# Stick-breaking attention on one core: the softplus total of later keys carried in one row of the next key block

## The chip, the cores and the metric

The kernel runs on one core of a Trainium2 chip. The metric is the device time of one execution in microseconds (us); for the kernel before, three runs gave 1367.43, 1368.22 and 1368.27, median 1368.22. A profile is one further execution, taken by the hardware profiler. In it, PE is TensorE (matmuls), PEld its weight loads, DVE VectorE, ACT ScalarE, POOL GpSimd, SP SyncE, which here only issues DMAs.

## The reference

One layer of a hybrid decoder: 1024 tokens, width 1024, everything in float32. A combined projection gives queries, keys and values (8 heads of 64), three inputs of a short convolution and two gates; both branches are merged, projected and normalised, and a feed-forward part follows. The change lies in the attention:

```python
z = jnp.einsum("bhqd,bhkd->bhqk", qb, kb).astype(jnp.float32) * scale
...
strict = s_idx < t_idx
log_keep = jnp.where(strict, jax.nn.log_sigmoid(-z), 0.0)
later = lax.cumsum(log_keep, axis=3, reverse=True) - log_keep
w = jnp.where(strict, jnp.exp(jax.nn.log_sigmoid(z) + later), 0.0)
outs.append(jnp.einsum("bhqk,bhkd->bhqd", w, vb.astype(jnp.float32)))
```

With sp(z) = log(1 + exp(z)), the weight of key s for query t is exp(z - S), where S is the sum of sp over the keys from s up to t - 1: the key itself and all later ones.

## The kernel before

Precision is kept by splitting each float32 operand into two 16-bit halves, high and low, and multiplying three of the four pairs (PASSES, L35). So most tiles that go into a matmul are made by two instructions: a copy on ACT (the high half) and a subtraction on DVE (the low half).

**Stages.** build() (L206) makes the constants, among them tri (L252 to L257): tri[:, 0] is 1 where the summed key is at or behind the key of the output row, tri[:, 1] its complement. mixer() (L264) loads and normalises the tokens x, transposes them into hT, projects v into four tiles v16 (v_out, L331), and q and k for four pairs of heads (qk_tile, L280; pair j holds two heads on 64 partitions each). The start, up to L501, has its order on PE, DVE and ACT written out by hand. Then come the four attention(j) (L591), after them the branches, the gates and the output projection, and ffn() (L990).

**Attention.** One pair has 12 units: for each half c of the queries (512 of them) the key blocks i of 128 keys, from the last that the half can see down to 0. A unit's tiles have 128 keys on the partitions and 2 x 512 columns (two heads, 512 queries); blocks on the diagonal are narrower by off (L595), so that the widths of both heads together are 256, 512, 768 and 1024 columns, then 1024 for all blocks below. stage1 (L602) makes z on PE, zc = min(scaled z, 44) with the causal mask on DVE, sp by Exp and Ln on ACT, and its halves sh. stage2 (L629) adds tri[:, 0] x sh to the PSUM tile A, which then holds S, makes zc - A on DVE, exp of it on ACT, and the halves w. stage2b (L647) adds the complement tri[:, 1] x sh, so that A holds the whole block's total in every row, ready for the next block. stage3 (L655) multiplies with v into o, which is copied into two halves o16 when a query half is finished (L668, L669).

**Order.** Program order is made by merge (L693): the loop at L673 runs stage1 of unit k, stage2 of unit k - 1, stage2b, and stage3 of unit k - 2, and between them it lets generators emit other matmuls: v tiles, q and k of the next pair, the convolution's inputs, in the last pair the first gate and four tiles of a branch (L707 to L720). What each engine runs in which order is then settled when the program is built, by a scheduler that keeps a timeline of its own and goes by priorities (high_priority at L609, L660, L675 to L685); an engine runs its list from front to back. Tiles come from pools with a fixed number of buffers: z, A and o have one, sp, sh and w two, zc three. A new tile waits until the last reader of the buffer's old tile is done. The table set that ACT uses for Exp and Ln together is loaded at L240; the sigmoid of the first gate (L786) and the gelu (L1240) use other sets. The weights' loads wait in SP's queue in program order.

Of the kernel before, what the change touches and what calls it, by code (L numbers as in the profile page):

```python
# [16 lines left out]
F16 = mybir.dt.float16  # L17
BF16 = mybir.dt.bfloat16
F32 = mybir.dt.float32
I32 = mybir.dt.int32  # L20
AF = mybir.ActivationFunctionType
ALU = mybir.AluOpType
AX = mybir.AxisListType

P = 128
# [9 lines left out]
PASSES = ((0, 0), (0, 1), (1, 0))  # L35


class Layer:
# [167 lines left out]
    def build(self):  # L206
# [23 lines left out]
        with ExitStack() as top:  # L230
# [24 lines left out]
            self.tri = c.tile([P, 2, P], F16, tag="tri", name="tri")  # L255
            nc.vector.tensor_copy(self.tri[:, 0, :], tri32)
            nc.vector.tensor_scalar(self.tri[:, 1, :], tri32, -1.0, 1.0, ALU.mult, ALU.add)  # L257
# [6 lines left out]
    def mixer(self, mid):  # L264
        tc, nc, a = self.tc, self.nc, self.a
        hT = self.hp.tile([P, 2, KD, T], F16, tag="hT", name="hT")
        with ExitStack() as ph1:
# [4 lines left out]
            self.clamp = att.tile([P, 2, NH], F16, tag="clamp", name="clamp")  # L272
            nc.gpsimd.memset(self.clamp, 44.0)
            nc.gpsimd.affine_select(self.clamp[:, :, :P], self.clamp[:, :, :P], [[0, 2], [1, P]], ALU.is_gt,
                                    -30000.0, base=0, channel_multiplier=-1)
            v16 = [self.slot([P, 2, 4, 4, 64], F16, f"v16_{i}") for i in range(4)]

            stk = {}

            def qk_tile(j, which):  # L280
# [12 lines left out]
                if which == "k":  # L293
                    cz = self.small(f"cz{j}", keep=True)
                    self.mul(cz[:, 0:1], s["iq"], inv)
                    self.mul(cz[:, 1:2], cz[:, 0:1], cst[:, 0:1])
                    s["cz"] = cz[:, 1:2]
# [3 lines left out]
            with tc.tile_pool(name="ptp", bufs=2, space=bass.MemoryType.PSUM) as ptp:  # L301
# [36 lines left out]
                def v_tile(tt):  # L338
# [9 lines left out]
                    v_out(tt, pv)  # L348

# [60 lines left out]
                with tc.manual_schedule(engines={ET.PE, ET.DVE, ET.Activation}):  # L410
# [51 lines left out]
                    v_out(1, pv[1])  # L462
                    square_x(5)
# [16 lines left out]
                    v_out(3, pv[3])  # L480
                    low(5)
# [109 lines left out]
            def attention(j):  # L591
# [10 lines left out]
                def stage1(u):  # L602
# [9 lines left out]
                    zc = att.tile([P, 2, NH], F32, tag="zc", name=f"zc{nm}", bufs=3)  # L612

                    if u["diag"]:
                        nc.vector.scalar_tensor_tensor(zc[:, :, off:], z[:, :, off:], s["cz"],  # L615
                                                       self.clamp[:, :, :NH - off], ALU.mult, ALU.min)
                    else:
                        nc.vector.tensor_scalar(zc[:, :, off:], z[:, :, off:], s["cz"], 44.0,
                                                ALU.mult, ALU.min)

                    sp = att.tile([P, 2, NH], F32, tag="sp", name=f"sp{nm}", bufs=2)
                    nc.scalar.activation(sp[:, :, off:], zc[:, :, off:], AF.Exp)  # L622
                    nc.scalar.activation(sp[:, :, off:], sp[:, :, off:], AF.Ln, bias=self.one)  # L623
# [3 lines left out]
                    u["zc"], u["sh"] = zc, sh  # L627

                def stage2(u):  # L629
                    off, i, c, nm, sh, zc = u["off"], u["i"], u["c"], u["nm"], u["sh"], u["zc"]  # L630
                    if u["top"]:
                        acc["A"] = pat.tile([P, 2, NH], F32, tag="A", name=f"A{nm}")
                    A = acc["A"]
                    for h in range(2):
                        for hl in range(2):
                            mm(A[:, h, off:], self.tri[:, 0, :], sh[:, hl, h, off:],
                               start=u["top"] and hl == 0, stop=False)
                    nc.vector.scalar_tensor_tensor(zc[:, :, off:], A[:, :, off:], -1.0, zc[:, :, off:],  # L638
                                                   ALU.mult, ALU.add)
                    nc.scalar.activation(zc[:, :, off:], zc[:, :, off:], AF.Exp)  # L640
                    w = att.tile([P, 2, 2, NH], F16, tag="w", name=f"w{nm}", bufs=2)
                    nc.scalar.activation(w[:, 0, :, off:], zc[:, :, off:], AF.Copy, scale=2.0 ** 14)  # L642
# [643 lines left out]
```

## Time and profile before

| | us |
|---|---|
| median of three runs | 1368.22 |
| the profiled execution, span from first to last instruction | 1365.7 |
| PE busy in the span | 1336.1 |
| DVE busy | 1028.6 |
| ACT busy | 860.7 |
| DVE low halves of sh (L626), 48 of them | 45.7 |
| DVE zc - A (L638), 48 of them | 45.5 |
| ACT Ln (L623), 48 of them | 44.6 |
| ACT exp (L640), 48 of them | 40.0 |

The span leaves out what lies before the first and behind the last instruction; the median of the runs is 2.5 us above it. A row of the timeline reads: start, duration, engine, line, operation, tile written <- tiles read, shape, number of instructions merged into the row, and in brackets how long the engine sat idle before it and what ended that. Numbers of buffers and pairs are left out of tile names, so zc stands for the zc of any unit. A row of a view by stretches reads: from:to, length, then the busy time of each engine with its number of instructions.

### The profile page before, as it was taken

How to read it: one execution, taken by the hardware profiler on the slowest of the kernel's cores; microseconds unless marked ns; L12 is line 12 of the kernel's file. 1: busy time of each engine (PE TensorE's matmuls, PEld its weight loads, DVE VectorE, ACT ScalarE, POOL GpSimd, SP SyncE). 2: the span in 40 equal slices, each digit the busy share in tenths (PEclk: the TensorE clock that was granted, in tenths of full speed). 3: DMA queues.
4: the chain of work that ended last, by engine and by line, in shares of the span. 5: the costliest groups of instructions: out<-in, count | busy, mean ns of one | idle time of the engine just before them, and what ended most of it. 6: DMA issues, size and time to landing. Idle time of an engine off the chain costs nothing. (4 is left out here: it accounts for less than half of the span.)

```text
span 1365.7 us, 16990 instructions
## 1 busy us (share of the span) xinstructions
PE 1336.1 (98%) x6651; PEld 607.7 (44%) x6651; DVE 1028.6 (75%) x1610; ACT 860.7 (63%) x1204; POOL 34.2 (3%) x52
## 2 busy tenths in 40 slices
PE   6999999999999999999999999999999999999997
PEld 3444444444444444444454444444444444444443
DVE  6667777777775965878788985984894896699855
ACT  6668778787775775666466577652761673476524
POOL 2000000000000000000010000000000000000002
PEclk9999999999999999999999999999999999999999
DMA  7102111101111121351331123122220321313216
GB/s 264 62 1 62 32 31 32 38 25 39 40 31 47 32 62 31 93 185 36 119 124 62 62 62 123 39 87 85 70 78 16 123 62 62 109 45 124 63 46 109
DMA packets 26576, 96.06 MB, mean 70 GB/s; under 512 B 3072, under 2 KB 3200, under 8 KB 26496
## 3 DMA queue, kind: packets, MB, share of 16 engines
q1 hardware_dynamic: 25056, 89.74, 20.3%
q0 software_dynamic: 1440, 5.24, 2.1%
q8 instruction: 52, 0.85, 0.2%
q14 instruction: 28, 0.23, 0.1%
HBM read 86.58 MB, written 8.39 MB: 70 GB/s over the span
## 5 line engine op out<-in xcount | busy, mean ns | idle before, releaser
L1156 PEld LDWEIGHTS <-wh_u 128*128 128x128 f16 x1848 | 178.8, 98 | 217.3 <-issue 3.5
L1048 PE MATMUL pd<-wdh,f 128*128 128x512 f16 (+1 forms) x1068 | 230.3, 377 | 2.8 <-ACT wdh L86 1.2
L1048 PEld LDWEIGHTS <-f 128*128 128x128 f16 x1068 | 104.4, 98 | 127.2 <-issue 4.3
L86 ACT ACTIVATE wh_u<-ws_u,sc 128x1024 f16<-128x1024 f32 (+1 forms) x66 | 64.7, 998 | 102.9 <-DVE sc L78 79.3
L1055 DVE SCALAR_TENSOR_TENSOR yacc<-pd,sd,yacc 128x512 f32<-128x512 f32 (+1 forms) x81 | 58.5, 740 | 72.7 <-PE pd L1048 65.2
L1156 PEld LDWEIGHTS <-wh_g 128*128 128x128 f16 x588 | 56.9, 98 | 68.7 <-issue 0.4
L859 PE MATMUL py<-wh_wo,m 128*128 128x512 f16 x384 | 83.9, 379 | 0.0
L87 DVE SCALAR_TENSOR_TENSOR wh_u<-ws_u,sc,wh_u 128x1024 f16<-128x1024 f32 (+1 forms) x66 | 72.1, 1099 | 9.5 <-ACT wh_u L86 9.4
L643 DVE SCALAR_TENSOR_TENSOR w<-zc,w 128x1024 f16<-128x1024 f32 (+3 forms) x48 | 45.7, 955 | 34.5 <-ACT w L642 34.4
L622 ACT ACTIVATE sp<-zc 128x1024 f32<-128x1024 f32 (+3 forms) x48 | 40.2, 838 | 46.7 <-DVE zc L615 29.1
L600 PE MATMUL A<-sh,tri 128*128 128x512 f16 (+3 forms) x352 | 67.8, 322 | 0.0
L1233 DVE SCALAR_TENSOR_TENSOR ugu<-cgu,cw_g,ugu 128x1023 f32<-128x1023 f32 (+1 forms) x44 | 56.2, 1278 | 11.3 <-ACT ugu L1231 10.9
L1233 DVE SCALAR_TENSOR_TENSOR ua<-cau,cw_a,ua 128x1023 f32<-128x1023 f32 (+1 forms) x44 | 56.1, 1276 | 1.4 <-ACT ua L1231 1.3
L859 PEld LDWEIGHTS <-m 128*128 128x128 f16 x384 | 37.5, 98 | 44.1
L626 DVE TENSOR_TENSOR sh<-sp,sh 128x1024 f16<-128x1024 f32 (+3 forms) x48 | 45.7, 952 | 12.9 <-ACT sh L625 12.7
L640 ACT ACTIVATE zc<-zc 128x1024 f32<-128x1024 f32 (+3 forms) x48 | 40.0, 834 | 15.4 <-DVE zc L638 15.0
L638 DVE SCALAR_TENSOR_TENSOR zc<-A,zc 128x1024 f32<-128x1024 f32 (+3 forms) x48 | 45.5, 949 | 2.3 <-PE A L600 2.3
L56 ACT ACTIVATE jk_u<-ws_u 128x1024 bf16<-128x1024 f32 x44 | 46.4, 1054 | 0.9
L200 PE MATMUL pk<-hT,wh_k 128*128 128x512 f16 x192 | 46.8, 380 | 0.0
L200 PE MATMUL pq<-hT,wh_q 128*128 128x512 f16 x192 | 44.3, 379 | 1.3 <-DVE sc L79 1.3
L623 ACT ACTIVATE sp<-sp,one 128x1024 f32<-128x1024 f32 (+3 forms) x48 | 44.6, 928 | 0.8
L200 PE MATMUL pcb<-hT,wh_cb 128*128 128x512 f16 x192 | 44.8, 379 | 0.0
(620 smaller groups left out, 2606.4 us busy)
## 6 DMA issues: line engine op xcount, KB each, us to landing
ws_u<-w_up_nt SPq DMA_DIRECT2D x44, 512.0 KB, 3.7
ds<-w_down SPq DMA_DIRECT2D x22, 512.0 KB, 6.1
wd<-w_down SPq DMA_DIRECT2D x22, 512.0 KB, 3.7
ws_g<-w_in_nt SPq DMA_DIRECT2D x14, 512.0 KB, 3.6
x<-x SPq DMA_DIRECT2D x8, 512.0 KB, 8.0
ws_wo<-w_out SPq DMA_DIRECT2D x8, 512.0 KB, 7.1
xr<-x SPq DMA_DIRECT2D x8, 512.0 KB, 4.3
out<-x SPq DMA_DIRECT2D x7, 512.0 KB, 2.9
```

The lines of the kernel that those rows point to most:

```text
L56: self.nc.scalar.activation(self.junk(f"jk_{name}"), src, AF.Square, accum_out=acc)
L86: self.nc.scalar.activation(dst[:, 0, :], src, AF.Copy, scale=s)
L87: self.nc.vector.scalar_tensor_tensor(dst[:, 1, :], src, s, dst[:, 0, :], ALU.mult, ALU.subtract)
L200: nc.tensor.matmul(ps, w[:, wi, ds(k * P, P)], hT[:, hi, k, ds(c * NH, NH)], start=n == 0, stop=n == last)
L600: nc.tensor.matmul(out, w, mv, skip_group_check=True, **kw)
L626: nc.vector.tensor_tensor(sh[:, 1, :, off:], sp[:, :, off:], sh[:, 0, :, off:], ALU.subtract)
L643: nc.vector.scalar_tensor_tensor(w[:, 1, :, off:], zc[:, :, off:], 2.0 ** 14, w[:, 0, :, off:], ALU.mult, ALU.subtract)
L859: nc.tensor.matmul(ps, m16[k][:, hi, ds(tt * P, P)], wo[k][:, wi, sl], start=k == 0 and p == 0, stop=k == 7 and p == 2)
L1048: nc.tensor.matmul(pd[nh], f16[g][k][:, hi, ds(tt * P, P)], w[k][:, wi, ds(*part)], start=run is runs[0] and n == 0, stop=run is runs[-1] ...
L1055: nc.vector.scalar_tensor_tensor(y[:, sl], ps, sm[:, 0:1], y[:, sl], ALU.mult, ALU.add)
L1156: nc.tensor.matmul(ps, w[wt][:, wi, ds(wc * NH + k * P, P)], self.block(i, hi, k), start=first and n == 0, stop=n == 3 * KH - 1, skip_grou ...
L1233: nc.vector.scalar_tensor_tensor(u[:, lag:], c[:, :T - lag], sm[:, 2 - lag:3 - lag], u[:, lag:], ALU.mult, ALU.add)
```

## The change

The order of two keys is changed in each block of 128: key 127, the last one, is put in row 96, and key 96 in row 127. For k this is a swap of two columns with three small copies on DVE; for v the two rows go out to DRAM and come back crossed, four DMAs for each of the four tiles. tri and the causal mask are built for this order, tri without its complement. As key 127 is the last of its block, what stands in its sp row enters the sums of all other rows. So the total of all later blocks, which is row 0 of their A, is added to row 96 of the next block's sp, and A is made anew for each unit by four matmuls. The weight is now the product of e = min(exp(z), 1.2e19) and g = exp(-A), where 1.2e19 stands for the old bound of 44 in the exponent. ACT takes exp(z) directly from the PSUM tile of z. In the loop, stage2 of unit k - 1 now stands ahead of a new stage1b of unit k, which adds the row and makes sh. e has three buffers, and g shares the two buffers of sp.

```diff
@@ -33,6 +33,7 @@
 GROUPS = (2, 4, 4, 4, 4, 4)
 KH = KD // 2
 PASSES = ((0, 0), (0, 1), (1, 0))
+EMAX = 1.2e19
 
 
 class Layer:
@@ -252,9 +253,14 @@
             tri32 = c.tile([P, P], F32, tag="tri32", name="tri32")
             nc.gpsimd.memset(tri32, 1.0)
             nc.gpsimd.affine_select(tri32, tri32, [[-1, P]], ALU.is_ge, 0.0, base=0, channel_multiplier=1)
-            self.tri = c.tile([P, 2, P], F16, tag="tri", name="tri")
-            nc.vector.tensor_copy(self.tri[:, 0, :], tri32)
-            nc.vector.tensor_scalar(self.tri[:, 1, :], tri32, -1.0, 1.0, ALU.mult, ALU.add)
+            q = slice(96, 128)
+            nc.gpsimd.memset(tri32[q, 96:97], 0.0)
+            nc.gpsimd.affine_select(tri32[q, 96:127], tri32[q, 96:127], [[0, 31]], ALU.is_ge, 0.0, base=30,
+                                    channel_multiplier=-1)
+            nc.gpsimd.memset(tri32[q, 127:128], 1.0)
+            nc.gpsimd.memset(tri32[96:97, :], 1.0)
+            self.tri = c.tile([P, P], F16, tag="tri", name="tri")
+            nc.vector.tensor_copy(self.tri, tri32)
 
             with ExitStack() as mid:
                 self.mixer(mid)
@@ -269,11 +275,22 @@
             pm = ph1.enter_context(tc.tile_pool(name="pm", bufs=3, space=bass.MemoryType.PSUM))
             self.sum_psum = (pm, [P, NH], "pm")
             att = pha.enter_context(tc.tile_pool(name="att", bufs=1))
-            self.clamp = att.tile([P, 2, NH], F16, tag="clamp", name="clamp")
-            nc.gpsimd.memset(self.clamp, 44.0)
-            nc.gpsimd.affine_select(self.clamp[:, :, :P], self.clamp[:, :, :P], [[0, 2], [1, P]], ALU.is_gt,
-                                    -30000.0, base=0, channel_multiplier=-1)
+            self.mask = att.tile([P, 2, P], F16, tag="mask", name="mask")
+            nc.gpsimd.memset(self.mask, 1.0)
+            nc.gpsimd.affine_select(self.mask, self.mask, [[0, 2], [1, P]], ALU.is_gt, 0.0, base=0,
+                                    channel_multiplier=-1)
+            nc.gpsimd.affine_select(self.mask[96:128, :, 97:], self.mask[96:128, :, 97:], [[0, 2], [0, 31]],
+                                    ALU.is_ge, 1.0, base=30, channel_multiplier=-1)
+            nc.gpsimd.memset(self.mask[96:97], 0.0)
+            dram = pha.enter_context(tc.tile_pool(name="vrow", bufs=1, space=bass.MemoryType.DRAM))
             v16 = [self.slot([P, 2, 4, 4, 64], F16, f"v16_{i}") for i in range(4)]
+
+            def swap_v(i):
+                rows = [dram.tile([1, 2, 4, 4, 64], F16, tag=f"vr{i}_{e}", name=f"vr{i}_{e}") for e in range(2)]
+                for e, r in enumerate((96, 127)):
+                    nc.sync.dma_start(rows[e], v16[i][r:r + 1])
+                for e, r in enumerate((127, 96)):
+                    nc.sync.dma_start(v16[i][r:r + 1], rows[e])
 
             stk = {}
 
@@ -291,6 +308,11 @@
                     nc.vector.scalar_tensor_tensor(s[which][:, 1, sl], ps, 2.0 ** -15, s[which][:, 0, sl],
                                                    ALU.mult, ALU.subtract)
                 if which == "k":
+                    kb = s["k"].rearrange("p h (b t) -> p h b t", t=P)
+                    kt = self.smp.tile([P, 2, KD, 1], F16, tag="kt", name=f"kt{j}", bufs=2)
+                    nc.vector.tensor_copy(kt, kb[:, :, :, 96:97])
+                    nc.vector.tensor_copy(kb[:, :, :, 96:97], kb[:, :, :, 127:128])
+                    nc.vector.tensor_copy(kb[:, :, :, 127:128], kt)
                     cz = self.small(f"cz{j}", keep=True)
                     self.mul(cz[:, 0:1], s["iq"], inv)
                     self.mul(cz[:, 1:2], cz[:, 0:1], cst[:, 0:1])
@@ -346,6 +368,8 @@
                             n += 1
                         yield
                     v_out(tt, pv)
+                    if tt % 2:
+                        swap_v(tt // 2)
 
                 load_x(0)
                 nc.sync.dma_start(gb, a["g_mix_pre"].broadcast_to([P, D]))
@@ -460,6 +484,7 @@
                     high(3)
                     low(3)
                     v_out(1, pv[1])
+                    swap_v(0)
                     square_x(5)
                     v_pass(2, range(8), PASSES, first=True, last=True)
                     rstd_x(5)
@@ -478,6 +503,7 @@
                     high(5)
                     norm_x(6)
                     v_out(3, pv[3])
+                    swap_v(1)
                     low(5)
                     self.wdone["v"] = wv, inv_wv
                     self.wpos = self.fpos = 3
@@ -609,48 +635,44 @@
                             with tc.high_priority(10 ** 6):
                                 mm(z[:, h, off:], s["k"][d, hk, ds(i * P, P)], s["q"][d, hq, tsl],
                                    start=n == 0, stop=n == 2)
-                    zc = att.tile([P, 2, NH], F32, tag="zc", name=f"zc{nm}", bufs=3)
-
+                    e = att.tile([P, 2, NH], F32, tag="e", name=f"e{nm}", bufs=3)
+                    nc.scalar.activation(e[:, :, off:], z[:, :, off:], AF.Exp, scale=s["cz"])
                     if u["diag"]:
-                        nc.vector.scalar_tensor_tensor(zc[:, :, off:], z[:, :, off:], s["cz"],
-                                                       self.clamp[:, :, :NH - off], ALU.mult, ALU.min)
-                    else:
-                        nc.vector.tensor_scalar(zc[:, :, off:], z[:, :, off:], s["cz"], 44.0,
-                                                ALU.mult, ALU.min)
-
+                        dg = slice(off, off + P)
+                        nc.vector.scalar_tensor_tensor(e[:, :, dg], e[:, :, dg], EMAX, self.mask, ALU.min, ALU.mult)
+                        off += P
+                    if off < NH:
+                        nc.vector.tensor_scalar(e[:, :, off:], e[:, :, off:], EMAX, None, ALU.min)
+                    off = u["off"]
                     sp = att.tile([P, 2, NH], F32, tag="sp", name=f"sp{nm}", bufs=2)
-                    nc.scalar.activation(sp[:, :, off:], zc[:, :, off:], AF.Exp)
-                    nc.scalar.activation(sp[:, :, off:], sp[:, :, off:], AF.Ln, bias=self.one)
+                    nc.scalar.activation(sp[:, :, off:], e[:, :, off:], AF.Ln, bias=self.one)
+                    u["e"], u["sp"] = e, sp
+
+                def stage1b(u):
+                    off, sp, nm = u["off"], u["sp"], u["nm"]
+                    if not u["top"]:
+                        A, o0 = acc["A"]
+                        nc.vector.tensor_tensor(sp[96:97, :, o0:], A[0:1, :, o0:], sp[96:97, :, o0:], ALU.add)
                     sh = att.tile([P, 2, 2, NH], F16, tag="sh", name=f"sh{nm}", bufs=2)
                     nc.scalar.activation(sh[:, 0, :, off:], sp[:, :, off:], AF.Copy)
                     nc.vector.tensor_tensor(sh[:, 1, :, off:], sp[:, :, off:], sh[:, 0, :, off:], ALU.subtract)
-                    u["zc"], u["sh"] = zc, sh
+                    u["sh"] = sh
 
                 def stage2(u):
-                    off, i, c, nm, sh, zc = u["off"], u["i"], u["c"], u["nm"], u["sh"], u["zc"]
-                    if u["top"]:
-                        acc["A"] = pat.tile([P, 2, NH], F32, tag="A", name=f"A{nm}")
-                    A = acc["A"]
+                    off, nm, sh, e = u["off"], u["nm"], u["sh"], u["e"]
+                    A = pat.tile([P, 2, NH], F32, tag="A", name=f"A{nm}")
+                    acc["A"] = A, off
                     for h in range(2):
                         for hl in range(2):
-                            mm(A[:, h, off:], self.tri[:, 0, :], sh[:, hl, h, off:],
-                               start=u["top"] and hl == 0, stop=False)
-                    nc.vector.scalar_tensor_tensor(zc[:, :, off:], A[:, :, off:], -1.0, zc[:, :, off:],
-                                                   ALU.mult, ALU.add)
-                    nc.scalar.activation(zc[:, :, off:], zc[:, :, off:], AF.Exp)
+                            mm(A[:, h, off:], self.tri, sh[:, hl, h, off:], start=hl == 0, stop=hl == 1)
+                    g = att.tile([P, 2, NH], F32, tag="sp", name=f"g{nm}", bufs=2)
+                    nc.scalar.activation(g[:, :, off:], A[:, :, off:], AF.Exp, scale=-1.0)
+                    nc.vector.tensor_tensor(g[:, :, off:], e[:, :, off:], g[:, :, off:], ALU.mult)
                     w = att.tile([P, 2, 2, NH], F16, tag="w", name=f"w{nm}", bufs=2)
-                    nc.scalar.activation(w[:, 0, :, off:], zc[:, :, off:], AF.Copy, scale=2.0 ** 14)
-                    nc.vector.scalar_tensor_tensor(w[:, 1, :, off:], zc[:, :, off:], 2.0 ** 14,
+                    nc.scalar.activation(w[:, 0, :, off:], g[:, :, off:], AF.Copy, scale=2.0 ** 14)
+                    nc.vector.scalar_tensor_tensor(w[:, 1, :, off:], g[:, :, off:], 2.0 ** 14,
                                                    w[:, 0, :, off:], ALU.mult, ALU.subtract)
                     u["w"] = w
-
-                def stage2b(u):
-                    if u["i"] > 0:
-                        off, sh = u["off"], u["sh"]
-                        for h in range(2):
-                            for hl in range(2):
-                                mm(acc["A"][:, h, off:], self.tri[:, 1, :], sh[:, hl, h, off:],
-                                   start=False, stop=False)
 
                 def stage3(u):
                     off, i, c, nm, w = u["off"], u["i"], u["c"], u["nm"], u["w"]
@@ -675,12 +697,13 @@
                         with tc.high_priority():
                             stage1(units[k])
                         yield 6
+                    with tc.high_priority():
+                        if 0 <= k - 1 < n:
+                            stage2(units[k - 1])
+                        if k < n:
+                            stage1b(units[k])
                     if 0 <= k - 1 < n:
-                        with tc.high_priority():
-                            stage2(units[k - 1])
                         yield 8
-                        with tc.high_priority():
-                            stage2b(units[k - 1])
                     if 0 <= k - 2 < n:
                         with tc.high_priority():
                             stage3(units[k - 2])
```

## The prediction

> **What bounds the kernel now.** The page first: TensorE (PE) is busy nearly throughout, the other engines are not.
>
> ```profile
> PE 1336.1 (98%) x6651; PEld 607.7 (44%) x6651; DVE 1028.6 (75%) x1610; ACT 860.7 (63%) x1204; POOL 34.2 (3%) x52
> ```
>
> An average hides stages, so the second view is the busy time of each engine in three stretches: the attention, the matmuls between its end and the next phase, the rest.
>
> ```profile
> core 0: us, PE busy (x) PEld busy (x) DVE busy (x) ACT busy (x) POOL busy (x), PEclk, DMA share, GB/s
> 62.00:411.00 349.00, 349.00 (x1993) 151.82 (x1992) 249.56 (x383) 265.83 (x355) 0.00 (x0) 1.00 0.12 35
> 411.00:443.54 32.54, 31.24 (x147) 14.10 (x148) 18.59 (x30) 16.72 (x21) 0.00 (x0) 1.00 0.16 49
> 443.54:1365.70 922.16, 908.77 (x4285) 416.46 (x4284) 720.17 (x1118) 538.10 (x772) 24.63 (x34) 1.00 0.26 78
> ```
>
> In the attention PE does not idle at all: the matmuls of projections, conv and gates ("filler") stand between those of the attention, whose chains through DVE and ACT wait unseen. The timeline shows how the cover ends:
>
> ```profile
> 410.16 0.84 PE L600 MATMUL o<-w,v 128*64 128x512 f16 x6
> 410.93 10.53 PE L200 MATMUL pga<-hT,wh_ga 128*128 128x512 f16 x48
> 443.54 0.16 PE L74 MATMUL pr<-rb,ones 128*128 128x1 bf16 x1 [1.30 <-DVE ywc L587]
> ```
>
> The last attention matmuls end at 411 with 32 us of filler (pga, four pywc tiles) still to come. What follows 443.5 needs the attention finished. So two things count: PE work saved, and whether the filler still outlasts the attention.
>
> **What is removed.** 160 of the 352 A matmuls (the complement sums): 64 of 512 columns and 32 each of 128, 256 and 384.
>
> ```profile
> 62.00:411.00 349.00, 67.76 (x352) 45.54 (x48) 1.00 0.12 35
> 393.15 1.89 PE L600 MATMUL A<-sh,tri 128*128 128x512 f16 x8
> 100.91 0.83 PE L600 MATMUL A<-sh,tri 128*128 128x128 f16 x8
> 166.46 1.26 PE L600 MATMUL A<-sh,tri 128*128 128x256 f16 x8
> ```
>
> The first row is the A tile alone: 67.76 us. A run of eight includes 0.17 us of one matmul's tail, so one costs (1.89-0.17)/8 = 0.215, 0.083 and 0.136 us; 384 columns lie between, 0.17. Removed: 64 x 0.215 + 32 x (0.083+0.136+0.17) = 26 us. Bounds: 24 (the 0.215 taken per column, 57,344 columns) and 30 (the share of columns in 67.76). I take 26.
>
> **What is added, and where it queues.** Per unit (a key block against 512 queries, two heads) DVE keeps four full operations, with min in place of zc, and gains the one-partition row add (40 of them) and, in diagonal units, a second piece of the min; ACT keeps five. The price is in the dependencies. Before, A stayed in PSUM from unit to unit, and one unit's softplus needed nothing of the unit ahead. Now the row add of unit k+1 reads A of unit k, and sh, its low half and A of unit k+1 wait for it. Buffers tie more: e has three, so exp(z) of unit k+3 waits for the product of unit k; g shares two buffers with sp, so Ln of unit k+2 waits until the low half of sh of unit k+1 is made.
>
> The program built from the change shows the consequence in its lists. On PE, filler runs out at the fifth-last unit of head pair 2: from the end of A of pair 2, block 4 (second query half), to the matmul that stood at 443.54, only 12 filler matmuls are left, beside 17 units' remaining products. The scheduler planned slower chains and used the filler earlier. On ACT, the sigmoids of the first gate, which ran at 416 us, now stand inside pair 2. After them the table set with Exp and Ln together is not reloaded; ACT's list holds 42 table loads instead of 3, 32 in this last stretch: one ahead of each Ln and one ahead of the Exp that follows.
>
> **Price of one unit there.** Full-width rows, then narrow ones:
>
> ```profile
> 388.08 1.28 DVE L618 TENSOR_SCALAR zc<-z,cz 128x1024 f32<-128x1024 f32 x1
> 390.48 1.15 ACT L623 ACTIVATE sp<-sp,one 128x1024 f32<-128x1024 f32 x1
> 391.54 1.04 ACT L640 ACTIVATE zc<-zc 128x1024 f32<-128x1024 f32 x1
> 392.61 1.06 ACT L642 ACTIVATE w<-zc 128x1024 f16<-128x1024 f32 x1
> 395.08 1.23 DVE L638 SCALAR_TENSOR_TENSOR zc<-A,zc 128x1024 f32<-128x1024 f32 x1 [0.16 <-PE A L600]
> 396.22 1.21 DVE L626 TENSOR_TENSOR sh<-sp,sh 128x1024 f16<-128x1024 f32 x1
> 396.34 1.06 ACT L640 ACTIVATE zc<-zc 128x1024 f32<-128x1024 f32 x1 [1.06 <-DVE zc L638]
> 380.72 0.82 PE L600 MATMUL z<-q,k 64*128 64x512 f16 x6
> 65.87 0.40 ACT L622 ACTIVATE sp<-zc 128x256 f32<-128x256 f32 x1
> 69.18 0.43 DVE L626 TENSOR_TENSOR sh<-sp,sh 128x256 f16<-128x256 f32 x1 [0.69 <-ACT sh L625]
> 70.57 0.62 ACT L622 ACTIVATE sp<-zc 128x512 f32<-128x512 f32 x1
> 418.40 0.58 ACT L668 ACTIVATE o<-o 128x512 f16<-128x512 f32 x1
> 410.82 4.26 ACT L86 ACTIVATE p<-pf,sc 128x1024 f16<-128x1024 f32 x4
> 414.98 1.14 ACT L86 ACTIVATE wh_wc<-ws_wc,sc 128x1024 f16<-128x1024 f32 x1
> 416.14 1.28 ACT L786 ACT_TABLE_LOAD   x1
> 417.43 1.06 ACT L786 ACTIVATE sgc<-sgc 128x1024 f32<-128x1024 f32 x1
> ```
>
> They show 0.03 us from DVE's end to ACT's start (396.31, 396.34), 0.09 us of overlap between neighbours on one engine, and 1.28 us for a load with nothing on either side (416.12, 416.14; 417.42, 417.43). The row add has no row; its width is that of the 1.23 operation on A in PSUM, and I take 1.22; free would be the lower bound.
>
> From the start of g = exp(-A): g to 1.06; product on DVE 1.09-2.31; exp(z) of the unit three on 2.34-3.40; w 3.31-4.37; sh 4.28-5.34; load to 6.62. DVE meanwhile: row add to 3.44, min to 4.71, low half of w to 5.84, low half of sh to 6.97. Now Ln, 7.0-8.15, load, 9.43: the next g starts (A was ready at 7.8). While A waits, all that PE has in its list behind it waits too: the next z and o. So 9.4 us a full unit, against 2.4 us of PE work (rows of six z 0.82 and six o 0.84 us, less tails, and four A).
>
> The 17 intervals, laid out likewise in the lists' order: pair 2 10.6, 10.0, 8.5, 7.2, 9.6; pair 3 6.7, 6.7, 7.6, 7.4, then 6.7, 7.5, 9.4, 9.3, 12.4, 8.2, 6.6, 7.3. A narrow one in full, pair 3, block 3 (256 columns): g to 0.40; product 0.43-0.86; exp(z) of the full block 0 0.89-1.95; w 1.86-2.26; sh of block 2 2.17-2.79; copy of pair 2's o 2.70-3.28; load 4.56; Ln of block 1 (768 columns, between the rows, 0.94) 5.50; load 6.78. Of the others, the two without a next unit's Ln spare the loads; 12.4 has four subtractions of the Strassen blocks queued ahead of its product on DVE; the last ends with both copies of o. Sum 141.7 us. PE's work in it is 33.1 us (z 7.9, A 11.4, o 11.2, 12 filler matmuls 2.6): idle 108.6. In the four units before, the same layout gives 42.7 us against 36.8 of PE work, since ACT and DVE also hold the four splits of p (the 4.26 us row): 6 more.
>
> Sum: -26 removed, -1.3 (the wait at 443.54 is absorbed), +108.6 + 6 = +87.3. The rest of the program follows in the same order, with PE dense, so the shift stays: span 1365.7 + 87 = 1453; the median lies 2.5 above the span, so 1455.
>
> A one-source fp32 operation held in SBUF, like min, may run at two elements a cycle by the Trainium skill (VectorE: DVE Perf Modes, Mode 2x_2P). The nearest row, 1.28 us, reads PSUM; no row here shows the mode, and the sum would be 1453 by it.
>
> **Covered edits.** The 16 row copies of v through DRAM are 4 KB each on SP's queue, ahead of loads of k2 and cc1.
>
> ```profile
> cmw<-conv_mix SPq DMA_DIRECT2D x1, 6.0 KB, 9.2
> 59.03 5.12 PE L343 MATMUL pv<-wh_v,hT 128*128 128x512 f16 x23
> 64.09 0.34 PE L600 MATMUL z<-q,k 64*128 64x128 f16 x6
> 1.09 0.96 POOL L273 MEMSET clamp<- 128x1024 f16 x1
> 5.90 0.55 POOL L171 TENSOR_TENSOR r_pre<-r_pre,neghalf 128x1 f32<-128x1 f32 x1 [2.91 <-DVE r_pre L170]
> ```
>
> At 9.2 us or less a leg they land before the first o that reads them, tens of us after v is written; uncovered, two legs would cost 18. Swapping columns of k (three small DVE copies a pair) needs both halves of k0, so the first z (64.1) moves to about 81 us (some 100 matmuls of 0.215 us after 59), behind second halves and v tiles that PE runs anyway; it is part of why the attention is late, and counted there. POOL's six small extra instructions stand in the 2.91 us idle ahead of the first norm, and a quarter of the clamp memset remains: nothing.
>
> **Rivals.**
> - Stalls earlier (slower still). The 32 units before the stretch are spaced 9.4 us on PE (from the first z at 81 to 443.5-1.3-26-33.1 = 383); a full one without loads takes 8.1. If two more filler operations of 1.2 us each cut into each of the 14 full ones, PE waits 34 us more: 1489. Against: now A waits nowhere on PE.
> - Loads that drain ACT: each costs its 1.28 us again. The same layout with 2.57 gives 45 more: 1500. Against: the 0.02 us gaps above. The Trainium skill (ScalarE: Activation LUTs, What ACT_TABLE_LOAD costs) puts a switch at 1283 ns plus about 1380 ns of drain; the trace shows the first part alone.
> - Loads hidden, or not executed as listed: a full unit then takes 8.1 us, and the layout 26 less: 1429. For: the first load lies in the wait for the low half; the second does not.
> - Faster: filler lasts as before, PE stays dense and only the 26 us count: 1342. It decides where a unit in the last stretch takes under 54/17 = 3.2 us; g, product, w and sh alone take 4.4. It needs another order on PE than the built one.
>
> **How the numbers follow.** Forecast 69 in 100, own range 1440 to 1472; stalls 13, drains 6, hidden loads 8, faster 3, cancelling by chance 1. Range 1430 to 1490: it takes in hidden loads and earlier stalls. Under 0.2% (2.7 us) nothing can be told from no change: faster 0.03, same 0.01, slower 0.96.
>
> **What would show it.** Right: PE dense to about 340 us, then thin for 140 to 185 us, to about 530; some 40 ACT_TABLE_LOAD rows; A about 42 us over 192 matmuls; g to g about 9.4 us in the last full units. Wrong: filler matmuls still standing after the last o; three table loads; full units under 6 us; PE idle spread over 80 to 340 us, which would be the stalls.

## The result and the profile after

The kernel after takes 1456.72 us (median, 1456.46 to 1457.25), the kernel before 1368.24 us (1367.43 to 1369.01) beside it: ratio 1.0647, 95% interval 1.0631 to 1.0662. The change costs 88.5 us. The span of the profiled execution is 1455.4 us, 89.7 more than before.

The page of the kernel after: busy time of each engine, then the slices for PE and for its granted clock.

```profile
PE 1340.9 (92%) x6491; PEld 598.5 (41%) x6491; DVE 1055.8 (73%) x1685; ACT 915.2 (63%) x1243; POOL 34.5 (2%) x58
...
PE   6999999999644369999999999999999999999998
...
PEclk9999999999855579999999999999999999999999
```

PE runs 160 matmuls fewer and is yet busy 4.8 us longer. The slices tell where both come from: in slices 11 to 15 (36.4 us each, so from 364 to 546 us) PE is thin, and in three of them the granted clock falls to little over a half. The stretches of the kernel after (from:to, length, busy PE, PEld, DVE, ACT, POOL, then the granted clock, DMA share and GB/s):

```profile
62.00:345.00 283.00, 282.22 (x1525) 121.01 (x1524) 187.69 (x343) 185.25 (x256) 0.00 (x0) 1.00 0.14 43
345.00:383.00 38.00, 36.66 (x194) 15.33 (x193) 26.01 (x51) 36.79 (x42) 0.00 (x0) 1.00 0.09 28
383.00:440.00 57.00, 25.40 (x109) 8.29 (x109) 31.21 (x38) 47.03 (x51) 0.00 (x0) 0.62 0.03 10
440.00:531.00 91.00, 38.65 (x151) 11.56 (x151) 60.16 (x66) 69.78 (x72) 0.00 (x0) 0.58 0.00 0
531.00:600.00 69.00, 69.00 (x320) 31.13 (x319) 45.80 (x66) 49.27 (x74) 0.00 (x0) 0.99 0.16 46
```

and of the kernel before, the first four in one:

```profile
62.00:531.00 469.00, 467.70 (x2548) 205.68 (x2547) 334.66 (x501) 345.70 (x468) 0.00 (x0) 1.00 0.13 38
```

From 62 to 531 us PE is idle for 469 - (282.22 + 36.66 + 25.40 + 38.65) = 86.1 us, before for 1.3. So 84.8 us of the 89.7 are new idle time, nearly all behind 383 us; the other 4.9 are the busy time: fewer matmuls, but those in the thin stretch at little over half the clock. From 531 us PE is dense again. Neither ACT nor DVE is full there either (ACT 116.8 of 148 us): it is a chain that sets the time. The ends of it on PE:

```profile
527.27 1.49 PE L626 MATMUL o<-w,v 128*64 128x512 f16 x6 [4.72 <-DVE w L673]
530.17 0.16 PE L75 MATMUL pr<-rb,ones 128*128 128x1 bf16 x1 [1.41 <-DVE o L691]
```

The matmul that stood at 443.54 stands at 530.17. The starts of g in the timeline of ACT give the chain's pace:

```profile
385.65 1.02 ACT L669 ACTIVATE g<-A 128x1024 f32<-128x1024 f32 x1
...
414.81 1.02 ACT L669 ACTIVATE g<-A 128x1024 f32<-128x1024 f32 x1
423.19 1.02 ACT L669 ACTIVATE g<-A 128x1024 f32<-128x1024 f32 x1 [3.49 <-PE A L626]
...
469.04 0.60 ACT L669 ACTIVATE g<-A 128x512 f32<-128x512 f32 x1
476.53 0.81 ACT L669 ACTIVATE g<-A 128x768 f32<-128x768 f32 x1
484.93 1.02 ACT L669 ACTIVATE g<-A 128x1024 f32<-128x1024 f32 x1
494.03 1.02 ACT L669 ACTIVATE g<-A 128x1024 f32<-128x1024 f32 x1
505.97 1.02 ACT L669 ACTIVATE g<-A 128x1024 f32<-128x1024 f32 x1 [0.47 <-PE A L626]
514.42 1.02 ACT L669 ACTIVATE g<-A 128x1024 f32<-128x1024 f32 x1
522.59 1.02 ACT L669 ACTIVATE g<-A 128x1024 f32<-128x1024 f32 x1 [3.48 <-PE A L626]
```

Seventeen intervals, from 385.65 to 530.17, 144.5 us. One of them in full, the timeline of all engines behind the g of 484.93:

```profile
485.99 1.23 DVE L670 TENSOR_TENSOR g<-e,g 128x1024 f32<-128x1024 f32 x1 [2.81 <-ACT g L669]
487.24 1.22 DVE L655 TENSOR_TENSOR sp<-A,sp 1x1024 f32<-1x1024 f32 x1
487.25 1.11 ACT L639 ACTIVATE e<-z,cz 128x1024 f32<-128x1024 f32 x1 [1.29 <-DVE g L670]
488.26 1.05 ACT L672 ACTIVATE w<-g 128x1024 f16<-128x1024 f32 x1
488.41 1.46 PE L626 MATMUL z<-q,k 64*128 64x512 f16 x6 [3.75 <-ACT e L639]
488.49 0.69 DVE L645 TENSOR_SCALAR e<-e 128x1024 f32<-128x1024 f32 x1
489.21 1.04 ACT L657 ACTIVATE sh<-sp 128x1024 f16<-128x1024 f32 x1
...
490.27 1.28 ACT L648 ACT_TABLE_LOAD   x1
...
490.48 1.22 DVE L658 TENSOR_TENSOR sh<-sp,sh 128x1024 f16<-128x1024 f32 x1
...
491.56 1.15 ACT L648 ACTIVATE sp<-e,one 128x1024 f32<-128x1024 f32 x1
...
492.11 0.82 PE L626 MATMUL A<-sh,tri 128*128 128x512 f16 x3
492.73 1.28 ACT L669 ACT_TABLE_LOAD   x1
```

ACT runs without a gap from exp(z) to the next g, both table loads within it; PE, in the middle of its work, waits 3.75 us for exp(z) to free z. A is done at 492.93, before the load ends at 494.01: in this unit the loads, not PE, come last.

### The profile page after: what moved, and what is told of

Its sections match the earlier page's. It is cut to its first block, busy times and chain, and to the rows that moved or that the text cites. A ratio compares the mean times of both kernels' runs of the same rounds, so it can differ in the third digit from the quotient of the medians.

```text
span 1455.4 us, 16839 instructions
## 1 busy us (share of the span) xinstructions
PE 1340.9 (92%) x6491; PEld 598.5 (41%) x6491; DVE 1055.8 (73%) x1685; ACT 915.2 (63%) x1243; POOL 34.5 (2%) x58
## 5 line engine op out<-in xcount | busy, mean ns | idle before, releaser
L670 DVE TENSOR_TENSOR g<-e,g 128x1024 f32<-128x1024 f32 (+3 forms) x48 | 45.9, 956 | 70.5 <-ACT g L669 70.5
L626 PE MATMUL A<-sh,tri 128*128 128x512 f16 (+3 forms) x192 | 55.2, 382 | 29.5 <-ACT sh L657 27.0
L626 PE MATMUL z<-q,k 64*128 64x512 f16 (+3 forms) x288 | 38.2, 377 | 46.0 <-ACT e L639 46.0
L639 ACT ACTIVATE e<-z,cz 128x1024 f32<-128x1024 f32 (+3 forms) x48 | 43.0, 897 | 32.8 <-DVE g L670 31.1
L669 ACT ACTIVATE g<-A 128x1024 f32<-128x1024 f32 (+3 forms) x48 | 38.7, 807 | 36.3 <-PE A L626 32.6
L626 PE MATMUL o<-w,v 128*64 128x512 f16 (+3 forms) x288 | 41.6, 406 | 8.4 <-DVE w L673 8.3
L648 ACT ACTIVATE sp<-e,one 128x1024 f32<-128x1024 f32 (+3 forms) x48 | 44.7, 931 | 6.9 <-DVE w L673 4.5
L673 DVE SCALAR_TENSOR_TENSOR w<-g,w 128x1024 f16<-128x1024 f32 (+3 forms) x48 | 45.8, 953 | 3.3 <-ACT w L672 3.1
L672 ACT ACTIVATE w<-g 128x1024 f16<-128x1024 f32 (+3 forms) x48 | 40.1, 835 | 9.8 <-DVE g L670 9.8
```

The lines of the kernel that those rows point to most:

```text
L626: nc.tensor.matmul(out, w, mv, skip_group_check=True, **kw)
L670: nc.vector.tensor_tensor(g[:, :, off:], e[:, :, off:], g[:, :, off:], ALU.mult)
L673: nc.vector.scalar_tensor_tensor(w[:, 1, :, off:], g[:, :, off:], 2.0 ** 14, w[:, 0, :, off:], ALU.mult, ALU.subtract)
```

## The experiments

All were run in three batches beside the kernel before (1368.14, 1368.40 and 1369.13 us, medians).

### Table loads (e1)

```diff
-                nc.scalar.activation(sig[which, 0], sig[which, 0], AF.Sigmoid)
+                one2 = self.small(f"one2{which}", keep=True)[:, 0:1]
+                nc.vector.tensor_scalar(one2, o16[3][:, 1, T - 1:T], 0.0, 1.0, ALU.mult, ALU.add)
+                nc.scalar.activation(sig[which, 0], sig[which, 0], AF.Sigmoid, scale=one2)
```

> The changed kernel, but the sigmoids of the first gate take their scale (1.0) from a number made of the last o16 of pair 3, so that they cannot stand inside the attention; ACT's list then has 3 table loads instead of 42. Theory (a chain through ACT and DVE sets the pace once the filler is used up, and the loads lie on it): 26 us less than the changed kernel, 1431. Rival, loads hidden in the wait for the low half of sh: 1455 to 1457. Rival, the loads are the whole loss: 1368 or less.

Measured: 1435.61 us, ratio 1.0492 (1.0477 to 1.0508), 21 us less than the kernel after, with 3 loads. So the loads lie on the path, and they are not all of it. Why 21 and not 26, a full unit of this kernel shows (timeline of ACT):

```profile
461.68 1.15 ACT L648 ACTIVATE sp<-e,one 128x1024 f32<-128x1024 f32 x1 [0.92 <-DVE w L673]
464.31 1.02 ACT L669 ACTIVATE g<-A 128x1024 f32<-128x1024 f32 x1 [1.48 <-PE A L626]
...
473.11 1.02 ACT L669 ACTIVATE g<-A 128x1024 f32<-128x1024 f32 x1 [1.99 <-PE A L626]
```

Where the second load stood, g now waits 1.5 to 2.0 us for A: a load that is taken away uncovers the next wait. The first row also says what Ln waits for: the low half of w (L673), not the low half of sh.

### The exchange of k's columns and v's rows (e2, e6)

In e2 the three copies of k are made after each half of the columns, not after both. In e6 nothing is exchanged.

```diff
+                    if which == "k":
+                        kb = s["k"][:, :, sl].rearrange("p h (b t) -> p h b t", t=P)
...
-                if which == "k":
-                    kb = s["k"].rearrange("p h (b t) -> p h b t", t=P)
```

> The changed kernel, but the columns of k are swapped half by half, each half as soon as its projection is done, so that the first z need not wait for the second half of k0. Theory (the attention is late as a whole, so its end moves with its start): the first z at about 64 us instead of 81, and the time 12 to 17 us less, 1440 to 1445. Rival, the start is hidden by matmuls that PE runs anyway: 1457.

> The changed kernel without any exchange of rows: neither the columns of k nor the rows of v are moved, so the keys are not in the order that tri is built for. Theory (the row copies of v through DRAM cost nothing, and the whole 13 us of the half-by-half exchange of k was the delay of the first z): 1440 to 1446, as with k exchanged half by half. Rival (the 16 row copies hold up SP's queue or the first o): 1425 to 1435. Rival 2 (the copies of k on DVE themselves cost, not the delay): under 1440, too, but with the first z at the same time as in the half-by-half kernel.

Measured: 1443.61 us (ratio 1.0552, 1.0536 to 1.0568) and 1443.43 us (1.0554, 1.0538 to 1.0570). First and last start of z, as the view of that tile gives them for the kernel after and for e2:

```profile
L626 PE MATMUL z<-q,k x288: 216/376/631, 80.0 to 489.2; 64*128 64x512 f16 x72, 64*128 64x128 f16 x24, 64*128 64x256 f16 x24, 64*128 64x384 f16 x24
```

```profile
L627 PE MATMUL z<-q,k x288: 213/376/632, 63.5 to 476.5; 64*128 64x512 f16 x72, 64*128 64x128 f16 x24, 64*128 64x256 f16 x24, 64*128 64x384 f16 x24
```

The first z comes 16.5 us earlier in e2, the last 12.7 us: that delay is worth 13 of the 88.5 us, as expected, although PE is dense at 64 us and far beyond. It is paid 300 us later, in filler that has been used up sooner; the 13 us include four table loads fewer (38 for 42). The row copies of v and the small copies of k cost nothing that can be measured.

### Both (e11)

> The changed kernel with the sigmoid held back (e1) and k exchanged half by half (e2) together; the order in the loop stays as changed. Theory (the two act separately, 21 and 13 us): 1420 to 1426. Rival (both only shorten the same uncovered stretch and one contains part of the other): 1428 to 1435.

Measured: 1420.72 us (1.0383, 1.0368 to 1.0399), 36 us less than the kernel after, against 21 + 13 = 34: the two add, within 2 us.

### The weights as a product, alone (e4)

The kernel before, complement sums and order kept, with the weights as e times g:

```diff
-                    nc.vector.scalar_tensor_tensor(zc[:, :, off:], A[:, :, off:], -1.0, zc[:, :, off:],
-                                                   ALU.mult, ALU.add)
-                    nc.scalar.activation(zc[:, :, off:], zc[:, :, off:], AF.Exp)
+                    g = att.tile([P, 2, NH], F32, tag="sp", name=f"g{nm}", bufs=2)
+                    nc.scalar.activation(g[:, :, off:], A[:, :, off:], AF.Exp, scale=-1.0)
+                    nc.vector.tensor_tensor(g[:, :, off:], e[:, :, off:], g[:, :, off:], ALU.mult)
```

> The kernel before with the new weights alone: e = min(exp(z), 1.2e19) times g = exp(-A), with the same mask and buffers as in the changed kernel; the complement sums stay, and no total is carried in a row. Theory (the product form costs nothing by itself, the filler still outlasts the attention): 1364 to 1372. Rival, the product form lengthens the chain enough to starve PE: above 1380.

Measured: 1371.47 us, ratio 1.0025 (1.0016 to 1.0034). This half of the change costs 3 us by itself. The stretch that the prediction took for the attention, in e4:

```profile
62.00:411.00 349.00, 349.00 (x1974) 149.65 (x1972) 238.82 (x396) 267.30 (x352) 0.00 (x0) 1.00 0.11 35
```

PE is as dense as before. The 3 us are busy time of PE, 1339.0 us for 1336.1 over the same 6651 matmuls; no run shows why.

### The complement sums, alone (e5)

```diff
-                        with tc.high_priority():
-                            stage2b(units[k - 1])
```

> The kernel before without its 160 complement matmuls, and nothing else; A then lacks part of the later blocks' sums, so the weights are not the reference's. Theory (those matmuls cost what was removed in the prediction, 26 us, while PE is dense throughout): 1342, plus or minus 4. Rival 1 (they stand partly in gaps that PE would have anyway): 1355 to 1366. Rival 2 (without them the chains of the attention become visible on PE and take the saving back): 1366 or more.

Measured: 1348.30 us, ratio 0.9857 (0.9842 to 0.9872): 20 us less, between the theory and its first rival. The busy time of the A tile (PE; then DVE's zc - A), the stretch in which PE idles, and the wait in it:

```profile
62.00:560.00 498.00, 43.59 (x192) 45.70 (x48) 0.99 0.14 43
```

```profile
380.00:400.00 20.00, 15.48 (x72) 6.37 (x69) 13.54 (x25) 19.89 (x21) 0.00 (x0) 0.91 0.07 25
```

```profile
397.22 0.58 PE L600 MATMUL A<-sh,tri 128*128 128x512 f16 x1 [4.39 <-ACT sh L625]
```

A fell from 67.76 to 43.59, by 24.2 us. Between 380 and 400 us PE idles 4.5 us, which it does not with the complement sums: the order of the kernel before, too, then shows a wait for ACT, which is busy for 19.9 of these 20 us. Two things can be behind it, and this run does not separate them: PE has 24 us less to do, and in e5 the sigmoids of the first gate have slipped in among the attention's functions, with 8 table loads in all for 3, three of them between 381.95 us and the copy that PE waits for.

### The row add and the order around it (e3, e7)

e3 adds into a row that is read by nothing, so sh no longer waits for it:

```diff
-nc.vector.tensor_tensor(sp[96:97, :, o0:], A[0:1, :, o0:], sp[96:97, :, o0:], ALU.add)
+nc.vector.tensor_tensor(self.mask32[96:97, :, o0:], A[0:1, :, o0:], sp[96:97, :, o0:], ALU.add)
```

> The changed kernel, but the row add writes its sum into a scratch row that nobody reads: every instruction stays, and sh of a unit no longer waits for A of the unit ahead. The totals of later blocks are left out of the weights. Theory (the dependency from unit to unit makes the loss): PE dense until about six units before the end, 1342 plus some 30 us of idle PE there, 1365 to 1385. Rival, the added DVE work (40 row adds, pieces of the min) makes it: above 1440.

Measured: 1401.83 us, ratio 1.0248 (1.0231 to 1.0265): 55 us less than the kernel after, but 17 to 37 more than expected. A unit of it (timeline):

```profile
434.10 1.02 ACT L670 ACTIVATE g<-A 128x1024 f32<-128x1024 f32 x1
435.15 1.22 DVE L671 TENSOR_TENSOR g<-e,g 128x1024 f32<-128x1024 f32 x1 [0.75 <-ACT g L670]
436.41 1.22 DVE L656 TENSOR_TENSOR rs<-A,sp 1x1024 f32<-1x1024 f32 x1
...
437.68 1.89 PE L627 MATMUL A<-sh,tri 128*128 128x512 f16 x4 [4.33 <-DVE rs L656]
...
443.33 1.02 ACT L670 ACTIVATE g<-A 128x1024 f32<-128x1024 f32 x1
```

The chain wasn't cut: A has one buffer, so the next A waits until the row add, queued behind the product on DVE, has read the old one. A unit takes 9.2 us as before. What became smaller is the number of such units: 100 attention matmuls run on PE behind the last filler, not 228, and with them the table loads, 26 for 42.

e7 keeps the arithmetic; what stage2 does from g on becomes stage2c, so that g, product and w of unit k - 1 stand behind the row add and sh of unit k:

```diff
                         if k < n:
                             stage1b(units[k])
+                        if 0 <= k - 1 < n:
+                            stage2c(units[k - 1])
```

> Same arithmetic as the changed kernel; only the program order in the loop: row add and sh of unit k now stand ahead of g, product and w of unit k - 1. The carried chain (A, row add, sh, low half, A) then no longer waits for the product on DVE or the w copy on ACT. Theory (the length of the carried chain in the last stretch is what costs, and with a shorter one the scheduler also leaves more filler): 1380 to 1405. Rival 1 (order inside the unit does not matter, ACT's and DVE's work per unit does): 1440 to 1457. Rival 2 (the early exhaustion of the filler alone costs): below 1370.

Measured: 1396.35 us, ratio 1.0211 (1.0194 to 1.0228), 60 us less than the kernel after, by an edit of the order alone, and in the range expected. Only a small part of it is a faster uncovered unit. The g of 512 columns in the second query half of pair 3, and the matmul behind the attention:

```profile
416.89 0.59 ACT L673 ACTIVATE g<-A 128x512 f32<-128x512 f32 x1
...
470.57 0.16 PE L75 MATMUL pr<-rb,ones 128*128 128x1 bf16 x1 [1.41 <-DVE o L695]
```

These last seven intervals take 53.7 us, in the kernel after 61.1 (469.04 to 530.17), both with ten table loads in them: 7 us less for the same units. The matmul behind the attention stands 60 us earlier; the rest comes from the units that are covered now, since 90 attention matmuls run behind the last filler in place of 228, and the loads in all are 26 for 42. So of the theory the second half (more filler is left) carries most of the gain, the first (a shorter chain in the last stretch) a small part.

### More PE work in the same stretch (e10)

This generator is appended, with n = 48, to the filler of the last pair:

```diff
+            def dummy(n):
+                ps = pm.tile([P, NH], F32, tag="pm", name="dummy")
+                for _ in range(n):
+                    for _ in range(8):
+                        nc.tensor.matmul(ps, self.tri, acts[0][0][:, 0, :NH], start=True, stop=True)
+                    yield
```

> The changed kernel with 384 matmuls of 512 columns added as the last filler of head pair 3, whose result nobody reads: about 83 us of PE work more. 36 attention matmuls instead of about 238 are left behind the last filler; the 42 table loads stay. Theory (in the stretch the chains through ACT and DVE set the time, PE has over 80 us to spare, and the lower granted clock there adds about 0.5 to 0.9 us to each unit): the granted clock stays near 1.0, six z take 0.82 us again, and the time is 1435 to 1457, no longer than without the 83 us of work. Rival 1 (the clock costs nothing on the chain): 1455 to 1465. Rival 2 (PE work adds up): 1500 to 1540.

Measured: 1465.87 us, ratio 1.0710 (1.0692 to 1.0728), 9 us more than the kernel after for 83 us of work more: above the theory's range, and 1 us above that of its first rival. The stretch 383 to 531 in the kernel after and in e10:

```profile
383.00:531.00 148.00, 64.05 (x260) 19.85 (x260) 91.38 (x104) 116.81 (x122) 0.00 (x0) 0.59 0.01 4
```

```profile
383.00:531.00 148.00, 124.35 (x628) 50.85 (x625) 87.34 (x100) 113.14 (x117) 0.00 (x0) 0.91 0.02 4
```

PE takes 368 matmuls more in the same 148 us, at a clock of 0.91 instead of 0.59. Rival 2 falls: PE had that time to spare. What the clock costs isn't settled. The groups of ACT show one thing that stood against a shorter time:

```profile
L669 ACT ACTIVATE g<-A 128x1024 f32<-128x1024 f32 (+3 forms) x48 | 38.7, 807 | 36.3 <-PE A L626 32.6 <-PE pr L75 2.2 <-DVE w L673 1.4
```

```profile
L676 ACT ACTIVATE g<-A 128x1024 f32<-128x1024 f32 (+3 forms) x48 | 38.7, 807 | 46.3 <-PE A L633 42.7 <-PE pr L75 2.2 <-DVE w L680 1.4
```

In the kernel after (first) g waits 32.6 us for A, in e10 42.7: the added matmuls stand ahead of z and A in PE's list, and those 10 us may cover what the higher clock gives.

### Versions that beat both (e8, e9)

e8 joins the edits of e1, e2 and e7 and gives e a fourth buffer (first two lines). e9 adds two of the tiles that stood behind the attention as filler:

```diff
-                    e = att.tile([P, 2, NH], F32, tag="e", name=f"e{nm}", bufs=3)
+                    e = att.tile([P, 2, NH], F32, tag="e", name=f"e{nm}", bufs=4)
...
-                    gens += [gate0("gc"), p_split(), gate0("ga")] + [branch(0, d, pm) for d in range(4, 8)]
-                    nf += 65
+                    gens += [gate0("gc"), p_split(), gate0("ga")] + [branch(0, d, pm) for d in (4, 5, 6, 7, 2, 3)]
+                    nf += 81
...
-            branches(2, 3, bi=0)
```

> Three edits that change no result put together: row add and sh ahead of g, the first gate's sigmoid held back until the attention's last o (3 table loads), k exchanged half by half; and a fourth buffer for e. 25 attention matmuls are left behind the last filler matmul in PE's list instead of about 238. Theory (the 26 us saved on PE are real and were outweighed only by the uncovered chains and loads): 1342 plus a few us of idle time, 1345 to 1360, faster than before. Rival (the carried chain costs inside the covered part, too): 1368 or more, with PE idle in many small pieces between 80 and 380 us.

> The kernel of e8 with two more tiles of the first branch (96 matmuls of 512 columns, about 21 us, which stood behind the attention) emitted as the last filler of head pair 3; 12 attention matmuls instead of 25 are then left behind the last filler in PE's list. Theory (the time that e8 still loses is PE's idle time between 416 and 435 us, where no filler is left): 10 to 16 us less than e8, 1346 to 1352. Rival (the last units' chains take longer when the filler's DVE and ACT work, the copies of the branch tiles, comes among them): 1358 to 1364, nothing gained.

Measured: e8 1362.22 us, ratio 0.9958 (0.9944 to 0.9973); e9 1351.91 us, ratio 0.9880 (0.9866 to 0.9895). The covered part and the end of the attention in e8, then the end in e9:

```profile
62.00:345.00 283.00, 282.60 (x1571) 118.26 (x1570) 219.14 (x384) 214.06 (x291) 0.00 (x0) 1.00 0.13 40
383.00:415.00 32.00, 32.00 (x164) 13.56 (x162) 29.66 (x40) 26.97 (x33) 0.00 (x0) 1.00 0.17 50
415.00:436.00 21.00, 7.29 (x31) 2.81 (x29) 20.90 (x20) 9.84 (x12) 0.00 (x0) 0.63 0.00 0
```

```profile
383.00:428.00 45.00, 45.00 (x227) 19.36 (x226) 41.67 (x59) 36.12 (x43) 0.00 (x0) 1.00 0.17 51
428.00:437.00 9.00, 3.56 (x20) 1.35 (x19) 8.97 (x9) 3.75 (x5) 0.00 (x0) 0.87 0.09 36
```

PE is dense until the filler ends in both, and idles 13.7 us behind it in e8, 5.4 in e9. e8 lies 2 us above the range expected of it, and below its rival's; e9 gained 10.3 us over e8, as expected. In the covered part the carried chain costs next to nothing on PE: 0.4 us of idle time up to 345. In another order, and with two more tiles as filler, the arithmetic of the change is thus 17 us faster than the kernel before. That kernel was not run with the added filler; it idles only 1.3 us between 62 and 531, so there is little for it to cover.

## Why the prediction was right

**The bound and the mechanism.** The prediction's first step, that two things count, PE work and whether the filler outlasts the attention, fits the variants of the changed kernel. The traces give the attention matmuls that PE runs behind the last filler, and the table loads:

| | matmuls behind the last filler | table loads | us |
|---|---|---|---|
| after | 228 | 42 | 1457 |
| e2 | 212 | 38 | 1444 |
| e3 | 100 | 26 | 1402 |
| e7 | 90 | 26 | 1396 |
| e1 | 231 | 3 | 1436 |
| e11 | 206 | 3 | 1421 |
| e8 | 25 | 3 | 1362 |
| e9 | 12 | 3 | 1352 |

With 26 loads or more (first four) and with 3 (last four) the time follows the count; in the first four the loads fall with it. The "about 238" of the expectations takes in ten matmuls that PE runs ahead of its last filler. e10, with 36, belongs in neither row, as its filler is added work.

**The saving, 26 us.** The A matmuls were worth 24.2 us (e5), at the lower bound of the prediction; 20 of it arrive even with the chains of before.

**Start and pace of the uncovered stretch.** Predicted: from 383, moved by 6 us of earlier idle time to 389, then 141.7 us, end near 530.8 (443.54 + 87.3). Measured: 385.65, 144.5 us, 530.17. The two errors cancel, which is luck: PE idled 2.1 us instead of 6 before 383, and the seventeen intervals were 2.8 longer. Fourteen of them are within 0.5 us of the layout. The three others:

| interval | predicted | measured | why |
|---|---|---|---|
| pair 2, 4th (414.81) | 7.2 | 8.38 | no load in it; g waits 3.49 for A |
| pair 3, 7th (476.53) | 9.4 | 8.40 | Ln did not wait for the low half of sh; min short |
| pair 3, 11th (514.42) | 6.6 | 8.17 | no load in it; g waits 3.48 for A |

**The rest of the program.** "With PE dense, so the shift stays": it grew, from 86.6 us at 530.17 to 89.7 at the end of the span. PE idles no more there than before, but is busy for 911.8 us in place of 908.8. 1.3 us of it lie in the first 48 matmuls behind the attention, which took 11.83 us for 10.52, with a granted clock of 0.69 from 531 to 534 us; where the rest comes from stays open. So the median agrees within 2 us partly by luck, too; the shape of the loss does not hang on it.

**Steps that failed within it.** "Ln waits for the low half of sh because g and sp share two buffers": at 491.56 Ln starts while that half is still being made (490.48 to 491.70), and e1's row names the low half of w. "min 1.28": it took 0.69. With both, the full unit shown was 0.3 us shorter than laid out (9.10 for 9.4). By the Trainium skill (VectorE: DVE Perf Modes, Mode 2×_2P) a one-source fp32 operation within SBUF may run at two elements a cycle; the trace agrees, 0.69 us beside 1.23 for the two-source product of the same shape. "A about 42 us over 192 matmuls": A took 55.2, and PE's work in the stretch 64 us instead of 33.1, since six z took 1.46 us in place of 0.82; so PE idled 84 us there, not 108.6, in nearly the predicted length. That the lower clock hardly moved the end is read from the unit shown, where A is done before the load that g needs; it may count where no load stands ahead of g, in two of the three rows of the table of intervals. No run shows its price; e10, which was to show it, does not. Two slips in the prediction's arithmetic change nothing: six z, six o and four A less their tails make 2.2 us by its rows, not 2.4, and the 1429 us of hidden loads lie just outside the range that is said to take them in.

**The loads.** The list of groups has, of 42,

```profile
L648 ACT ACT_TABLE_LOAD x18 | 23.1, 1283 | 0.3
L669 ACT ACT_TABLE_LOAD x16 | 20.5, 1283 | 0.3
```

18 ahead of Ln and 16 ahead of g, the Exp that follows, as the prediction had it; there are 0.02 us to either neighbour in the unit shown (490.25 to 490.27, 491.55 to 491.56), so the rival of a draining ACT falls. Worth 21 us (e1) where the prediction had 26 for the step from hidden to visible loads: behind a load stood A.

**Covered edits.** v's row copies: nothing, as predicted (e6). k's columns: z at 80.0 for a predicted 81, and 13 us of the total (e2), which the prediction counted in the lateness of the attention without giving it a price. The row add: 1.22 us as taken. The product: about 3 us (e4) by itself; the prediction gave it no price.

**Rivals.** Earlier stalls: PE busy 282.22 of 283 us up to 345. Hidden loads: 1429 would have asked for e1 to change nothing. Faster (1342) needed another order on PE than the built one; e7 to e9 made one, and e9 came to 1352.

## What to carry to other kernels

Independent matmuls that hide a chain are a stock that is spent: an edit that delays or lengthens the chain can cost nothing where it stands and be paid where the stock runs out, so read from the program's own list what stands behind the last filler. A result that is carried from step to step should be taken, and passed on, ahead of all other work of the step. And a table load that a scheduler lets slip among functions of another set can repeat at every step; one scale taken from a late tile holds it back.

## What the runs showed of the hardware

**The granted clock follows use.** With PE busy in 64 of 148 us, in bursts with gaps such as the 3.75 and 4.72 us shown, the mean granted clock was 0.59; with 124 of 148 us it was 0.91. The six z behind the gap of 3.75 us took 1.46 us, 1.8 times the 0.82 of the kernel before. The Trainium skill (TensorE: Matmul & The Clock Gate, the part on the clock gate) states a half clock after an idle window of some 3.4 us, and full clock after one that is busy; the rows agree, if means of 0.58 to 0.63 are taken for stretches with both.

**One partition cost as much as 128.** The row add, 1x1024 elements with one source in PSUM, took 1.22 us, the product of 128x1024 in SBUF 1.23.
